# List matmuls ordered behind the dense products, the first listed unit one place later, and one modulation group moved from one block to the next

## The chip, the cores and the metric

The kernel runs on one core of one Trainium2 chip. The metric is the device time of one execution in microseconds; the profiled execution also gives a span, from the first to the last instruction of the trace.

## The reference, cut to what matters

Two layers on 256 positions of width 1024. Each layer is a mixer (layer 0 retention, layer 1 a spatial-gating unit) followed by a PEER expert retrieval over 128 x 128 experts. Every part has an adaptive modulation: six groups (shift, scale, gate, twice) that come from `c`.

```python
c_act = jax.nn.silu(c)
mod = c_act @ ada_w[layer] + ada_b[layer]
sh1, sc1, g1, sh2, sc2, g2 = jnp.split(mod, 6, axis=-1)   # groups 0 to 5
x = x + g1 * mixer(modulate(rmsnorm(x), sh1, sc1))
x = x + g2 * peer_ffn(modulate(rmsnorm(x), sh2, sc2), ...)
# peer_ffn: two top-16 lists per head give 16 experts of 16384 per head and token
a = gelu(einsum('tkd,td->tk', expert_u[idx], x)) * gate
return einsum('tk,tkd->td', a, expert_v[idx])
```

## The kernel before, in words

Float32 products are made of three matmuls each: an operand is split into `hi` (L162, ScalarE) and `lo = raw - hi` (L163, VectorE), and `hi*hi`, `hi*lo` and `lo*hi` are summed in PSUM. Weights come in tiles of 128 x 1024, loaded by SyncE's queue (L159) in a fixed order, `AHEAD = 2` tiles ahead of use, with three buffers for `raw`, `hi` and `lo`.

**PEER, up to the V products.** The 128 x 128 experts are held as 128 rows of 128. The activations of all experts are computed densely and multiplied by a dense table of gates. For the first `N0 = 72` rows the products go to a table in DRAM (`w_dram`, from tile `A`, in eight pieces); for the other 56 rows the activations go to `a_dram` and the gates stay in `G`.

**The V products.** They walk over 60 units (`peer_v_order`). 28 are natural: two whole expert rows, `at` reloaded from `a_dram` (L1051), multiplied by `G` (L1082), split into `wh` and `wl` (L1073, L1074), and 24 matmuls of 512 columns (L392). The other 32 are listed: expert cells that any token uses are packed into 64 columns; a unit of kind "b" (15) has 24 matmuls, of kind "x" (17) 12 (L1089). Each listed unit is fetched by four indirect DMAs from GpSimd (L168): two of `vraw` (weights) and two of `cell` (gated activations). They may run up to five units ahead (`DEEP + 1`). The first `FIRST = 16` units are natural, the remaining 12 are mixed among the listed ones, and one "b" comes last.

**The sorter.** Which cells are listed is worked out while the natural units run, by a generator `sort_rows`, of which each of the first `SORTED = 14` units advances one step: three steps of flags; masks, in a pool that takes the space of `A` and so waits until it was written out (`open_lists`, L915); `numbers`, with one matmul (L931) between VectorE operations; `lists`, with nine chunks of eight small matmuls (L984), each chunk needing `pm` and `eq` (L973, L977, VectorE), `cm` of its rows (L980, GpSimd) and of its columns (L982, ScalarE); then the indices `vi` and `agi` (L1018), which the gathers need; and a count (L1028, L1030) that SyncE and the other engines read for a branch (L1140). At unit 14 what is left of the sorter is emitted at once, and the gathers may begin.

**The modulation.** `ada(layer, ks)` is a generator that works out groups `ks`: for each group eight loads of 128 x 1024 (L287, SyncE's queue), eight VectorE operations (L289, L291), eight transposes on TensorE (L299) and two reductions (L300). It is advanced one step at a time between products. In layer 0's V products the groups (0,5), (1,1), (1,0) and (1,2) are made, in layer 1's group (1,5), and in layer 1's gating unit (1,4) and (1,3).

**The gating unit's output stage.** After the input projection (`z_group`) come `gate_rows(1, 2)`, which spreads group (1,2) over rows by eight VectorE operations `dg` (L375, two buffers) and eight transposes (L376), and then eight groups of spatial products (L207 to L209, `u` at L648), transposes (L658, `ph` and `pl` at L453, L454) and three output products each.

**Order.** The program's order is not the order on the engines: a scheduler simulates the program and places an instruction on its engine's queue when the simulation has it ready. `after_mark(inst, mark, ORDER)` keeps `inst` behind `mark` in that order, without a wait. `marks["pe"]` is the last product emitted so far. Engines then work through their queues in order.

Of the kernel before, what the change touches and what calls it, by code (L numbers as in the profile page):

```python
# [44 lines left out]
CAP = (17, 30, 17)  # L45
NC = sum(CAP)
BASE = (0, CAP[0], CAP[0] + CAP[1])
FIRST = 16
SORTED = 14
DEEP = 4  # L50


# [72 lines left out]
def trunk(ctx: ExitStack, tc: tile.TileContext, I, out):  # L125
# [449 lines left out]
    def sgu(xt, pool, update):  # L575
# [62 lines left out]
                nc.scalar.copy(vh[:, b, s], v)  # L638
                nc.vector.tensor_tensor(vl[:, b, s], v, f(vh[:, b, s]), op=ALU.subtract)
        accs = acc_tiles()  # L640
        filler = ada(1, (4, 3), hpool, "hl", "hh")

        def spatial(g):
            s = slice(g * GD, (g + 1) * GD)
# [16 lines left out]
                         ph[:, :, bs_], pl[:, :, bs_])  # L661
            return [(ph[:, e, :], pl[:, e, :]) for e in range(3)]

        grow = gate_rows(1, 2)
        spatial(0)
        spatial(1)
        nxt = turn(0)
        for g in range(GRP):
            if g + 2 < GRP:
                spatial(g + 2)  # L670
            cur, nxt = nxt, turn(g + 1) if g + 1 < GRP else None
            keys = [("sgu_out", g * 3 + e) for e in range(3)]
            if g == GRP - 1:
                drain(filler)
                out_group(accs, cur, keys)
            else:
                for e in range(3):
                    out_proj(accs, *cur[e], weight(*keys[e]), g == 0 and e == 0)
                    next(filler, None)
        return accs, grow  # L680

    def peer(layer, xt, hh, hl, xstack):
# [239 lines left out]
        def numbers(masks, caps, bases, pool, ps):  # L922

            n = len(caps)
            scan = pool.tile([P, n, n0], F32, tag="scan", name=nm("scan"))
            for c in range(n):
                nc.vector.tensor_tensor_scan(scan[:, c], ones[:, :n0], masks[:, c], 0.0,
                                             op0=ALU.mult, op1=ALU.add)
            sums = pool.tile([P, n], F16, tag="sums", name=nm("sums"))
            nc.vector.tensor_copy(sums, scan[:, :, n0 - 1])  # L930
            nc.tensor.matmul(ps[:, :n], listed["below"], sums, start=True, stop=True)  # L931
            off = pool.tile([P, n], F32, tag="off", name=nm("off"))
            nc.vector.tensor_copy(off, ps[:, :n])
            place = pool.tile([P, n0], F32, tag="place", name=nm("place"))
            left = pool.tile([P, n0], F32, tag="left", name=nm("left")) if n > 1 else None
            keep = pool.tile([P, n0], F32, tag="keep", name=nm("keep"))
            for c in range(n):
                pos = scan[:, c]
                nc.vector.tensor_scalar(pos, pos, off[:, c:c + 1], -1.0, op0=ALU.add, op1=ALU.add)
                nc.vector.scalar_tensor_tensor(keep, pos, float(caps[c] * P), masks[:, c],  # L940
                                               op0=ALU.is_lt, op1=ALU.mult)
                dst = place if c == 0 else pos
                nc.vector.scalar_tensor_tensor(dst, pos, float((bases[c] + 1) * P), keep,
                                               op0=ALU.add, op1=ALU.mult)
                if c:
                    nc.vector.tensor_tensor(place, place, pos, op=ALU.add)
                if n == 1:
                    continue
                d2 = left if c == 0 else keep
                nc.vector.tensor_tensor(d2, masks[:, c], keep, op=ALU.subtract)  # L950
                if c:
                    nc.vector.tensor_tensor(left, left, keep, op=ALU.add)
            return place, left

        def lists(place, ncol, pool, ps):

            ip = pool.tile([P, n0], U32, tag="ip", name=nm("ip"))
            iq = pool.tile([P, 2, n0], U32, tag="iq", name=nm("iq"))
            ih = pool.tile([P, 2, n0], F16, tag="ih", name=nm("ih"))
            nc.vector.tensor_copy(ip, place)  # L960
            nc.vector.tensor_scalar(iq[:, 0], ip, 127, None, op0=ALU.bitwise_and)
            nc.vector.tensor_scalar(iq[:, 1], ip, 7, None, op0=ALU.logical_shift_right)
            nc.vector.tensor_copy(ih, iq)
            yield
            ps = ps[:, :2 * ncol].rearrange("p (v c) -> p v c", v=2)

            def pairs(row, width):
                return row.rearrange("p (q e) -> p q e", e=2).unsqueeze(2) \
                    .to_broadcast([P, 4, width, 2])

            for i in range(0, n0, 8):
                pm = pool.tile([P, 4, P, 2], F16, tag="pm", bufs=2, name=nm("pm"))
                nc.vector.tensor_tensor(pm, iota_h.unsqueeze(1).to_broadcast([P, 4, P, 2]),  # L973
                                        pairs(ih[:, 0, i:i + 8], P), op=ALU.is_equal)
                cm = pool.tile([P, 4, 2, ncol, 2], F16, tag="cm", bufs=2, name=nm("cm"))
                eq = pool.tile([P, 4, ncol, 2], F16, tag="eq", bufs=1, name=nm("eq"))
                nc.vector.tensor_tensor(  # L977
                    eq, listed["cols"][:, :ncol].unsqueeze(1).to_broadcast([P, 4, ncol, 2]),
                    pairs(ih[:, 1, i:i + 8], ncol), op=ALU.is_equal)
                nc.gpsimd.tensor_tensor(cm[:, :, 0], eq, pairs(listed["rows"][:, i:i + 8], ncol),  # L980
                                        op=ALU.mult)
                nc.scalar.mul(cm[:, :, 1], eq, pidx)  # L982
                for k in range(8):
                    nc.tensor.matmul(ps, pm[:, k // 2, :, k % 2], cm[:, k // 2, :, :, k % 2],  # L984
                                     start=i + k == 0, stop=i + k == n0 - 1)
                yield
            row = pool.tile([P, ncol], F32, tag="row", name=nm("row"))
            nc.vector.tensor_copy(row, ps[:, 1])
            nc.vector.scalar_tensor_tensor(row, ps[:, 0], float(P), row, op0=ALU.mult, op1=ALU.add)
            v = pool.tile([P, ncol], I32, tag="vi", name=nm("vi"))  # L990
            nc.vector.tensor_scalar(v, row, float((layer * P - 1) * P), 0.0,
                                    op0=ALU.add, op1=ALU.max)
            yield row, v

        def sort_rows():
            for i in range(0, n0, 24):
                flag(1, i, 15, nc.vector)
                flag(1, i + 15, 9, nc.scalar)
                yield
            code, second = flags  # L1000
            nc.vector.tensor_scalar(second, second, 0.0, 2.0, op0=ALU.is_gt, op1=ALU.mult)
            nc.vector.scalar_tensor_tensor(code, code, 0.0, second, op0=ALU.is_gt, op1=ALU.add)
            open_lists()
            lp = listed["pool"]
            masks = lp.tile([P, 3, n0], F32, name=nm("masks"))
            for k, value in enumerate((1.0, 3.0, 2.0)):
                nc.vector.tensor_scalar(masks[:, k], code, value, None, op0=ALU.is_equal)
            yield
            place, left = numbers(masks, CAP, BASE, lp, ps_tile())
            yield  # L1010
            for got in lists(place, NC, lp, ps_tile()):
                yield
            row, listed["v"] = got
            agi = lp.tile([P, NC], I32, name=nm("agi"))
            one, two, three = (slice(BASE[c], BASE[c] + CAP[c]) for c in range(3))
            nc.vector.tensor_scalar(agi[:, one], row[:, one], 2.0, None, op0=ALU.mult)
            nc.vector.tensor_copy(agi[:, two], row[:, two])
            nc.vector.tensor_scalar(agi[:, three], row[:, three], 2.0, 1.0,  # L1018
                                    op0=ALU.mult, op1=ALU.add)
            listed["w"] = agi  # L1020
            yield
            listed["left"] = left
            count = lp.tile([P, 1], F32, name=nm("count"))
            nc.vector.tensor_reduce(count, left, axis=AX.X, op=ALU.add)
            ch = lp.tile([P, 1], F16, name=nm("ch"))
            nc.vector.tensor_copy(ch, count)
            ps = ps_tile()
            nc.tensor.matmul(ps[:1, :2], ch, ones_h, start=True, stop=True)  # L1028
            ci = lp.tile([1, 2], I32, name=nm("ci"))
            nc.vector.tensor_copy(ci, ps[:1, :2])  # L1030
            listed["count"] = ci
            yield

        accs = acc_tiles()
        if layer == 0:
            adag = chain(ada(0, (5,), hpool, "hl", "hh"), ada(1, (1, 0, 2), hpool, "hl", "hh"))
        else:
            adag = ada(1, (5,), hpool, "hl", "hh")
        order = peer_v_order()
# [83 lines left out]
        for pos, unit in enumerate(order):  # L1123
            wh, wl = nxt
            kind, c = unit
            if pos < SORTED:
                next(sorter, None)
            elif pos == SORTED:
                drain(sorter)
                listed["rows_pool"] = vstack.enter_context(  # L1130
# [148 lines left out]
```

## Time and profile before

| | |
|---|---|
| time, median of 3 runs | 2169.87 us (2166.07 to 2176.35) |
| time of the profiled execution | 2171.77 us |
| its span | 2170.0 us |
| TensorE matmul busy | 1993.5 us (92%) |
| VectorE busy | 1685.8 us (78%) |
| ScalarE, GpSimd busy | 1121.7 us (52%), 571.1 us (26%) |
| mean granted TensorE clock | 0.964 of full |

The page gives busy time per engine as a share of the span. "PE" is TensorE's matmuls, "PEld" its weight loads, "DVE" VectorE, "ACT" ScalarE, "POOL" GpSimd, "SP" SyncE; a "q" behind an engine is its sequencer or DMA queue. A wait is idle time of an engine, put down to what ended it. Line numbers are those of the kernel before.

### The profile page before, as it was taken

To read this page: it belongs to the slowest core of one execution; us is meant where nothing else is said; L and a number is where in the kernel's file an instruction comes from. 1 tells how busy PE (TensorE), PEld (TensorE's weight loads), DVE (VectorE), ACT (ScalarE), POOL (GpSimd) and SP (SyncE) were. 2 spreads that over 40 slices of the span, in tenths; PEclk is the share of its full clock that TensorE was granted. 3 is DMA by queue.
4 is the path that set the end of the run, shared out by engine and by line. 5 is a ranking of instruction groups with operands and counts; after the bars stand their busy time and mean duration, and the time that the engine had idled before them with its cause. 6 is when DMAs were issued, how large, how long until landed. Compare 5 with 4: busy or idle time off the path is not lost. (4 is left out here: it accounts for less than half of the span.)

```text
span 2170.0 us, 35151 instructions
## 1 busy us (share of the span) xinstructions
PE 1993.5 (92%) x12988; PEld 1777.3 (82%) x12988; DVE 1685.8 (78%) x3064; ACT 1121.7 (52%) x1894; POOL 571.1 (26%) x523
## 2 busy tenths in 40 slices
PE   4999899999999598899889899999999995988997
PEld 4988799999989476677677787999999894766785
DVE  7877678988988676678678777789989886666675
ACT  3444444446887444445454434444467874444553
POOL 1000001101010435877001700011010104448770
PEclk8999999999999799999999999999999997999999
DMA  7677456665575677899646865566555756777893
GB/s 267 213 256 263 162 177 185 183 183 183 181 248 190 228 233 256 277 335 357 214 154 214 256 230 189 176 182 183 184 181 189 247 189 230 233 246 241 299 299 111
DMA packets 137019, 478.72 MB, mean 221 GB/s; under 512 B 17408, under 2 KB 19472, under 8 KB 136320
## 3 DMA queue, kind: packets, MB, share of 16 engines
q1 hardware_dynamic: 94320, 335.85, 48.0%
q0 software_dynamic: 38192, 131.04, 18.2%
q10 hardware_dynamic: 4320, 9.44, 1.2%
q8 instruction: 105, 1.72, 0.3%
q14 instruction: 82, 0.67, 0.1%
HBM read 439.30 MB, written 36.96 MB: 219 GB/s over the span
## 5 line engine op out<-in xcount | busy, mean ns | idle before, releaser
L162 ACT CAST hi<-raw 128x1024 fp32r<-128x1024 f32 x536 | 561.5, 1049 | 643.4 <-PE ps L208 337.4
L163 DVE TENSOR_TENSOR lo<-raw,hi 128x1024 fp32r<-128x1024 f32 x536 | 683.1, 1277 | 123.8 <-ACT hi L162 121.0
L207 PE MATMUL ps<-hh,hi 128*128 128x256 f32 x2432 | 699.3, 288 | 11.6 <-ACT hi L162 7.8
L208 PE MATMUL ps<-hl,hi 128*128 128x256 f32 x2432 | 691.7, 285 | 1.6 <-DVE hl L358 1.4
L209 PE MATMUL ps<-hh,lo 128*128 128x256 f32 x2432 | 691.1, 285 | 1.7 <-DVE lo L163 1.5
L207 PEld LDWEIGHTS ps<-hh,hi 128*128 128x128 f32 x2432 | 468.7, 193 | 13.5 <-ACT hi L162 8.5
L208 PEld LDWEIGHTS ps<-hl,hi 128*128 128x128 f32 x2432 | 468.9, 193 | 2.4 <-DVE hl L358 2.4
L209 PEld LDWEIGHTS ps<-hh,lo 128*128 128x128 f32 x2432 | 468.3, 193 | 2.6 <-DVE lo L163 2.6
L163 DVE TENSOR_TENSOR lo<-vraw,hi 128x1024 fp32r<-128x1024 f32 x128 | 156.1, 1225 | 98.2 <-ACT hi L162 97.8
L392 PE MATMUL acc<-lo,wh 128*128 128x512 f32 x672 | 217.1, 404 | 4.8 <-DVE lo L163 4.7
L162 ACT CAST hi<-vraw 128x1024 fp32r<-128x1024 f32 x128 | 134.1, 1050 | 152.5 <-DMA vraw<-in_peer_v,vi 78.7
L392 PE MATMUL acc<-hi,wl 128*128 128x512 f32 x672 | 210.8, 395 | 0.0
L392 PE MATMUL acc<-hi,wh 128*128 128x512 f32 x672 | 193.5, 402 | 4.9 <-ACT wh L1073 3.3
L168 POOL DMA_INDIRECT cell<-w_dram,agi x128 | 167.3, 1307 | 39.0 <-issue 33.5
L759 POOL TENSOR_TENSOR eq<-eq,tif 128x512 f32<-128x512 f32 x32 | 56.7, 1786 | 449.8 <-DVE eq L754 403.8
L168 POOL DMA_INDIRECT vraw<-in_peer_v,vi x128 | 145.9, 1140 | 73.2 <-DVE agi L1018 33.6
L392 PEld LDWEIGHTS acc<-hi,wh 128*128 128x128 f32 x672 | 126.6, 190 | 35.7 <-ACT wh L1073 3.5
L392 PEld LDWEIGHTS acc<-lo,wh 128*128 128x128 f32 x672 | 124.1, 190 | 36.9 <-DVE lo L163 10.3
L392 PEld LDWEIGHTS acc<-hi,wl 128*128 128x128 f32 x672 | 126.1, 188 | 30.2
L907 POOL DMA_DIRECT2D a_dram<-at x56 | 30.6, 546 | 374.6 <-ACT at L802 228.8
L208 PE MATMUL ps<-lo,hh 128*128 128x512 f32 x320 | 125.8, 393 | 3.4 <-DVE lo L163 3.4
L209 PE MATMUL ps<-hi,hl 128*128 128x512 f32 x320 | 125.6, 392 | 0.0
(275 smaller groups left out, 2844.5 us busy)
## 6 DMA issues: line engine op xcount, KB each, us to landing
raw<-in_peer_u SPq DMA_DIRECT2D x256, 512.0 KB, 3.7
raw<-in_peer_v SPq DMA_DIRECT2D x112, 512.0 KB, 4.9
adaw<-in_ada_w SPq DMA_DIRECT2D x96, 512.0 KB, 5.3
raw<-in_sgu_in SPq DMA_DIRECT2D x48, 512.0 KB, 4.6
w_dram<-A POOLq DMA_DIRECT2D x16, 1152.0 KB, 14.4
raw<-in_ret_vg SPq DMA_DIRECT2D x32, 512.0 KB, 4.4
raw<-in_peer_q SPq DMA_DIRECT2D x32, 512.0 KB, 3.7
a_dram<-at POOLq DMA_DIRECT2D x56, 256.0 KB, 3.4
```

The source lines that it names most:

```text
L162: after_mark(nc.scalar.copy(hi, raw), after[0], ORDER)
L163: after_mark(nc.vector.tensor_tensor(lo, raw, f(hi), op=ALU.subtract), after[1], ORDER)
L168: nc.gpsimd.indirect_dma_start(out=dst, out_offset=None, in_=table, in_offset=bass.IndirectOffsetOnAxis(ap=index, axis=0))
L207: first = nc.tensor.matmul(ps, ah, bh, start=start, stop=False)
L208: nc.tensor.matmul(ps, ah, bl, start=False, stop=False)
L209: marks["pe"] = nc.tensor.matmul(ps, al, bh, start=False, stop=stop)
L392: marks["pe"] = nc.tensor.matmul(accs[b][n], a[:, tb], bb[:, n * 512:(n + 1) * 512], start=first and a is lh and bb is wh, stop=False)
L759: nc.gpsimd.tensor_tensor(eq, eq, tif[:, :, a, :].unsqueeze(2).to_broadcast([P, NTB, TOPK, TOPK]), op=ALU.mult)
L907: nc.gpsimd.dma_start(a_dram[:, sp * 2:sp * 2 + 2, :], tmp)
```

## The change

`FIRST` becomes 17 and `SORTED` 13: 17 natural units stand ahead of the first listed one, eleven are mixed among them, and the gathers are emitted from unit 13 on. The sorter takes two steps instead of one at units 5, 7, 9 and 11. The matmul of `numbers`, that of the count and the first of each chunk of the lists are kept behind the last dense product emitted before them; a chunk's matmuls are emitted in the step after the one that prepares its operands. `cm` of the rows moves from GpSimd to VectorE, and `eq` gets a second buffer. Group (1,2) leaves layer 0's V products and becomes the first of three groups in layer 1's output stage, with one more step behind most groups, and `gate_rows(1, 2)` moves from ahead of the spatial products to the end of output group 2.

```diff
-FIRST = 16
-SORTED = 14
+FIRST = 17
+SORTED = 13
...
-        filler = ada(1, (4, 3), hpool, "hl", "hh")
+        filler = ada(1, (2, 4, 3), hpool, "hl", "hh")
...
-        grow = gate_rows(1, 2)
         spatial(0)
         spatial(1)
...
                     out_proj(accs, *cur[e], weight(*keys[e]), g == 0 and e == 0)
                     next(filler, None)
+                    if e == 2 and g == 2:
+                        grow = gate_rows(1, 2)
+                    elif e == 2 and g:
+                        next(filler, None)
...
-            nc.tensor.matmul(ps[:, :n], listed["below"], sums, start=True, stop=True)
+            after_mark(nc.tensor.matmul(ps[:, :n], listed["below"], sums, start=True, stop=True),
+                       marks["pe"], ORDER)
...
-                eq = pool.tile([P, 4, ncol, 2], F16, tag="eq", bufs=1, name=nm("eq"))
+                eq = pool.tile([P, 4, ncol, 2], F16, tag="eq", bufs=2, name=nm("eq"))
...
-                nc.gpsimd.tensor_tensor(cm[:, :, 0], eq, pairs(listed["rows"][:, i:i + 8], ncol),
+                nc.vector.tensor_tensor(cm[:, :, 0], eq, pairs(listed["rows"][:, i:i + 8], ncol),
                                         op=ALU.mult)
                 nc.scalar.mul(cm[:, :, 1], eq, pidx)
+                yield
                 for k in range(8):
-                    nc.tensor.matmul(ps, pm[:, k // 2, :, k % 2], cm[:, k // 2, :, :, k % 2],
-                                     start=i + k == 0, stop=i + k == n0 - 1)
-                yield
+                    after_mark(nc.tensor.matmul(
+                        ps, pm[:, k // 2, :, k % 2], cm[:, k // 2, :, :, k % 2],
+                        start=i + k == 0, stop=i + k == n0 - 1),
+                        marks["pe"] if k == 0 else None, ORDER)
...
-            nc.tensor.matmul(ps[:1, :2], ch, ones_h, start=True, stop=True)
+            after_mark(nc.tensor.matmul(ps[:1, :2], ch, ones_h, start=True, stop=True),
+                       marks["pe"], ORDER)
...
-            adag = chain(ada(0, (5,), hpool, "hl", "hh"), ada(1, (1, 0, 2), hpool, "hl", "hh"))
+            adag = chain(ada(0, (5,), hpool, "hl", "hh"), ada(1, (1, 0), hpool, "hl", "hh"))
...
             if pos < SORTED:
-                next(sorter, None)
+                for _ in range(1 + (pos > 3 and pos % 2)):
+                    next(sorter, None)
```

## Rows read from the trace of the kernel before

**Rows 1.** Waits of PE over the whole span, longest in total: us, times, longest.
```profile
PE ps L931 <- DVE sums L930: 25.8, 2, 12.9
PE ps L984 <- POOL cm L980: 17.9, 2, 8.9
PE acc L1089 <- ACT wh L1073: 15.1, 2, 7.7
```

**Rows 2.** Stages: busy us (x instructions) of each engine, PE clock, DMA share, GB/s.
```profile
722.00:746.00 24.00, 1.27 (x10) 1.03 (x10) 11.47 (x41) 3.98 (x6) 5.92 (x7) 0.59 0.77 282
746.00:842.00 96.00, 95.87 (x445) 74.33 (x446) 67.30 (x70) 42.95 (x52) 38.10 (x36) 0.98 0.65 205
842.00:1072.00 230.00, 208.69 (x868) 161.39 (x867) 174.10 (x190) 112.51 (x134) 153.56 (x127) 0.96 0.89 310
980.00:1040.00 60.00, 59.40 (x259) 47.66 (x259) 50.41 (x55) 34.10 (x40) 41.26 (x37) 1.00 1.00 368
1928.00:2140.00 212.00, 193.72 (x808) 152.03 (x808) 138.54 (x153) 107.11 (x128) 153.81 (x127) 0.96 0.80 271
1250.00:1328.00 78.00, 76.86 (x365) 63.32 (x365) 61.08 (x74) 29.96 (x40) 0.00 (x0) 0.99 0.69 230
```

**Rows 3.** Timeline of all engines at the start of layer 0's V products.
```profile
732.49 0.29 DVE L915 TENSOR_SCALAR below<-iota_f,pidx 128x128 f16<-128x128 f32 x1 [11.17 <-DMA w_dram<-A]
733.91 0.55 POOL L1051 DMA_DIRECT2D at<-a_dram  x1 [11.06 <-DMA a_dram<-at]
...
741.89 1.42 POOL L980 TENSOR_TENSOR cm<-eq,rows_h 128x512 f16<-128x512 f16 x1 [5.40 <-DVE eq L977]
...
743.27 1.26 POOL L1082 TENSOR_TENSOR at<-at,G 128x512 f32<-128x512 f32 x1
...
745.48 0.60 ACT L1073 CAST wh<-at 128x512 fp32r<-128x512 f32 x1
...
746.13 1.22 PE L392 MATMUL acc<-hi,wh 128*128 128x512 f32 x2 [1.67 <-ACT wh L1073]
```

**Rows 4.** Tile `at`, 730 to 775 us: issue to landing of its loads.
```profile
DMA to landing us min/median/max: 2.9/3.0/4.1
```

**Rows 5.** Timeline of PE, 829 to 862 us: a list chunk, the gathers' wait.
```profile
831.05 0.63 PE L984 MATMUL ps<-cm,pm 128*128 128x128 f16 x8
831.49 0.71 PE L392 MATMUL acc<-hi,wh 128*128 128x512 f32 x2
832.04 0.63 PE L392 MATMUL acc<-lo,wh 128*128 128x512 f32 x2
832.50 0.62 PE L392 MATMUL acc<-hi,wl 128*128 128x512 f32 x2
...
850.36 1.22 PE L1089 MATMUL acc<-hi,wh 128*128 128x512 f32 x2 [7.43 <-ACT wh L1073]
...
861.46 0.63 PE L1089 MATMUL acc<-hi,wh 128*128 128x512 f32 x2
```

**Rows 6.** Timeline of POOL: first and last of layer 0's 128 gathers.
```profile
836.87 1.04 POOL L168 DMA_INDIRECT vraw<-in_peer_v,vi  x1 [16.30 <-DVE agi L1018]
...
1032.47 0.94 POOL L168 DMA_INDIRECT vraw<-in_peer_v,vi  x1 [0.30 <-issue]
```

**Rows 7.** Tile `eq`: VectorE's operation on it, ns min/median/max.
```profile
L977 DVE TENSOR_TENSOR eq<-cols_h,ih x18: 410/425/1518, 741.4 to 1903.1; 128x512 f16<-128x512 f16 x18
```

**Rows 8.** Waits of PE, 840 to 1070 us: us in total, times, longest.
```profile
PE acc L1089 <- ACT hi L162: 4.7, 2, 4.2
```

**Rows 9.** Waits of SP's queue, 700 to 760 us.
```profile
SPq L1140 <- DVE ci L1030: 6.3, 1, 6.3
```

**Rows 10.** Timeline, 1236 to 1262 us: PE at the gating unit's output stage.
```profile
1242.35 0.48 PE L376 MATMUL ps<-ident,dg 128*128 128x128 f32 x1 [5.11 <-DVE dg L375]
...
1250.13 1.22 PE L392 MATMUL acc<-hi,ph 128*128 128x512 f32 x2
```

**Rows 11.** VectorE's groups, shapes apart, 1237 to 1328 us: busy us, mean ns.
```profile
L291 DVE SCALAR_TENSOR_TENSOR ada<-adaw,c_act,ada 128x1024 f32<-128x1024 f32 x14 | 17.9, 1281 | 2.9 <-DMA adaw<-in_ada_w 1.8 <-PE ps L209 1.0
```

## The prediction, as it was put on record

> **What bounds the kernel now.** I read the page first: TensorE is busy for 92% of the span, so only stretches in which it stands still, and changes of its clock, can pay. The list of TensorE's waits comes next [rows 1]: three of its longest belong to the lines of this change, each twice, once a layer, and nearly alike in both layers (half of each total is about its longest). So I work out layer 0 and carry it to layer 1. The stage windows then say which parts of the V products have slack. Between the last u product and the first dense product TensorE is busy for 1.3 of 24 us; while the natural units run it is full (95.9 of 96 us); in the part with listed units it idles 21.3 of 230 us in layer 0 and 18.3 of 212 us in layer 1 [rows 2]. What the lists cost inside the full part therefore matters, and what hides beside it doesn't.
>
> The timeline of the start shows why TensorE waits. VectorE is held until 732.5 us by the write of `A`, and the reload of the first natural unit is issued at 733.9. It takes 3.0 us to land [rows 4], so its data are there at 736.9. But GpSimd does the first list chunk's `cm` at 741.9 before it multiplies the reload by `G` at 743.3, and TensorE has the matmul of `numbers` and the first eight list matmuls in its queue ahead of the products; the first product starts at 746.1 [rows 3]. At the other end, the gathers begin at 836.9 us, when `agi` is ready, and the first gathered product starts at 850.4, 13.5 us later, after a wait of 7.4 us and at half rate (1.22 us for two matmuls, where two later take 0.63: TensorE's lower clock level, 1.2 GHz, instead of 2.4; the granted clock averages 0.59 over the idle start) [rows 2, 5, 6].
>
> **The start of the V products.** Afterwards TensorE's queue holds the products of four units ahead of `numbers`, and GpSimd has no `cm`. The chain of the first product is then the load (736.9), the multiplication by `G` (1.26, to 738.2) and the cast `wh` (0.60, to 738.8): start at 738.9, 7.2 us earlier [rows 3, 4]. VectorE is free from 732.5, more than four microseconds before the reload lands, for the masks and the `lo` of the first rows; I take that as no bound. The eight list matmuls that ran in the idle time now stand among the products, where a chunk takes 0.44 us (831.05 to 831.49) [rows 5]. Gain 6.8 us a layer, 13.5 in all; nothing at the lower end, if the order on VectorE or GpSimd keeps list work ahead.
>
> **The first gathers.** A unit of 24 products takes 5.6 us (two per 0.46 to 0.47 us [rows 5]). Seventeen units, 72 list matmuls (9 x 0.44 = 4.0) and a half-rate start that costs 3.7 (before, 16 units and eight chunks make 93.1 us and took 96.8, from 746.1 to the 842.9 that lies 7.4 ahead of 850.4 [rows 3, 5]) end at 738.9 + 95.2 + 4.0 + 3.7 = 841.8. The ninth list chunk is emitted in unit 11's steps, behind the products of 11 units: its own matmuls and the eight before it included, 738.9 + 61.6 + 3.7 + 4.0 = 808.2. Before, 5.4 us lay between the end of the last chunk and the first gather (831.5 to 836.9); so gathers start at about 813.6, 28 us ahead of use instead of 6. They need 13.5, so the wait goes, and with it the half rate behind it: 850.36 to 861.46 holds one "x" and one "b", 36 products, 8.4 us at full rate, so 2.7 are lost [rows 5]. Gain 7.4 + 2.7 in layer 0 and 7.7 + 2.7 in layer 1 [rows 1]: 20.5.
>
> **The rest of the listed part.** In layer 0, 21.3 - 7.4 = 13.9 us of idle time are left, in layer 1 18.3 - 7.7 = 10.6 [rows 1, 2]; the largest is a wait for a gathered row's `hi` (4.7 us in two waits) [rows 8]. GpSimd issues 128 gathers from 836.9 to 1033.4 without a pause: 1.53 us each, 6.1 us a listed unit [rows 6]. TensorE needs 5.6 us for a "b" and 2.8 for an "x", and only the 12 natural units between them give GpSimd time: 15 x 5.6 + 17 x 2.8 + 12 x 5.6 = 199 us against 196. The two are even, so GpSimd can't make up a late start, and 15 us more of lead (28 less 13.5) cover as much of the lateness. Half-rate stretches behind the longest waits add some 2.5 us a layer, by the one above. I take 60% of 16.4 in layer 0, where the DMA share is 0.89, and 75% of 13.1 in layer 1, where it is 0.80 [rows 2]: 9.8 + 9.8 = 19.6. The bounds are nothing and 29.5.
>
> **What a list chunk costs now.** On VectorE `cm` is an operation of the size of `eq`, 0.42 us alone and up to 1.52 beside GpSimd's work [rows 7]: 9 x 0.42 = 3.8 us a layer, or 13.7. VectorE is busy for 67 of 96 us there [rows 2], so both fit. I take the lower, since GpSimd loses the work that it would collide with. The Trainium skill ("GPSIMD Engine Reference", section "8. Key points") says that GpSimd shares its memory interfaces with VectorE when VectorE has two inputs in SBUF, which speaks against a move to an engine with no interface of its own; the trace bears it out in the 1518 ns beside the 410 [rows 7]. By that rule alone the sum would hold 13.7 us a layer of VectorE time, still hidden.
>
> Where a unit takes two steps, a chunk's matmuls are held only behind the products that held the chunk before it, and TensorE may reach them before `cm` is there: three chunks a layer, at most about 4.4 us each, nothing at best. (The 4.4 are an estimate: two operations of 1.5 [rows 7], and 0.7 each for `pm`, twice as wide as `eq`, and for ScalarE's part.) Natural products queue behind it. In the full part before, eight chunks cost no wait [rows 2], so I take 0.5 each, 3 us. The count now becomes ready 13 units later, and SyncE's read of it (6.3 us before, in the idle start [rows 9]) holds the row loads behind it. Rows are loaded about three ahead, so I take 0.5 a layer, 1 us; 6.3 at the worst. One natural unit more is reloaded through ScalarE's queue and multiplied on VectorE: hidden. New waits: 4 us.
>
> **The moved group.** Eight loads of 512 KB, eight VectorE operations, eight transposes and two reductions leave layer 0's listed part and enter layer 1's output stage; TensorE's share is equal on both sides. In layer 0 it is 4.2 MB less, which is why I go to 60% above. In the output stage the first product runs at 1250.1, behind a wait of 5.1 us for a `dg` that sits in VectorE's queue behind the last weights, and at half rate [rows 10]. Without `gate_rows` there it can start some 5.5 us earlier. But VectorE is busy for 61 of the 78 us that follow [rows 2], and gets eight operations of 1.28 [rows 11], two reductions and the eight `dg`: 10 us and, as an estimate from these operations' smaller sizes, 4 more, so 75 of about 73 to 78. It becomes as long as TensorE's own work, and its waits give back the gain. I take nothing, with 6 us either way.
>
> **Sum.** 13.5 + 20.5 + 19.6 - 4 + 0 = 49.6 us. From the profiled execution's 2171.8 that is 2122; it lies 1.9 above the median of the runs, so the forecast is 2121.
>
> **Rivals.** *The transfers bind the listed part.* With TensorE at full rate (980 to 1040 us) the DMA engines are busy all the time, at 368 GB/s [rows 2]. Then an earlier start only makes the same bytes wait elsewhere, and the 19.6 are lost: 2121 + 20 = 2141. For it speaks that share; against it, that layer 0 loses 4.2 MB and layer 1 ran at 271 GB/s with almost as much idle time. The Trainium skill ("DMA: Bandwidth & Descriptors", section "Issuing engines are not separate DMA queues") has this rule: transfers of all queues run on the same 16 engines and interleave. The trace agrees, with a share of 1.00.
>
> *The output stage becomes VectorE's.* If its bursts can't be hidden, TensorE waits for most of the added 14 us, less the 5.5: about 9 us worse, 2130. A gap of 1.6 us stands there even now (78 - 76.9 [rows 2]).
>
> *The list matmuls hold the products* (the other side). TensorE works in order; if the scheduler places each chunk where its `cm` is only being prepared, all 18 wait. At 4.4 us each that is 79 us, less the 53.6 gained: 2170 + 25 = 2195. From 3 us each it is slower than before. Against it: none did so in the full part before.
>
> *It doesn't do what it says.* The order binds only TensorE's queue; VectorE's and GpSimd's may still put list work ahead, and the start stays, while the fetches go no further ahead than before: 2160 to 2172.
>
> **Chances and range.** The forecast 0.56, the transfers 0.17, the output stage 0.13, no effect 0.07, the list matmuls 0.07. The forecast's own range is 2101 (all of the 29.5, no new wait, 6 us in the output stage) to 2130; the range takes in the first two rivals to 2149, with a few us of new waits on top. Less than 0.5%, some 11 us, can't be told from no change here. Faster by more: 0.86; within: 0.08; slower: 0.06.
>
> **What would show it.** In the profile after: the first dense product about 5 us behind the reload's issue instead of 12; the first list matmul behind four units; no wait of L1089 for `wh`; `agi` some 28 us ahead of the first gathered product; GpSimd waiting for buffers between gathers, a sign that it leads. Against it: waits of TensorE for `cm` in the full part; the same idle time behind the first gathered unit at a DMA share near 1; VectorE above 95% in the output stage with TensorE waiting for `u`, `pl` or `lo`.

## The result, and the profile after

The changed kernel takes 2108.8 us (median of 4 runs, 2107.36 to 2110.9) against 2170.79 us for the kernel before on the same chip (4 runs, 2166.07 to 2176.35): ratio 0.9714, 95% interval 0.9689 to 0.974. It is 62 us faster; 49.6 were forecast. Two runs, one of e11 below (2146.47 us) and one of the kernel before on the same chip (2204.12 us), lay over 1.5% above the fastest run of their kernel and are left out.

I cut both traces at four landmarks, so that each stretch holds one idea of the change: the first dense V product of either layer, the first matmul of the norm (L337) that follows layer 0, and the same for the norm between the gating unit and the second PEER part.

| stretch, us | before | after | gain |
|---|---|---|---|
| start to first V product, layer 0 | 746.1 | 737.6 | 8.5 |
| V products, layer 0, to the next norm | 349.0 | 315.8 | 33.2 |
| gating unit, norm to norm | 241.4 | 251.3 | -9.9 |
| PEER of layer 1 up to its first V product | 495.1 | 487.5 | 7.6 |
| V products, layer 1, to the end | 338.4 | 315.5 | 22.9 |
| span | 2170.0 | 2107.7 | 62.3 |

TensorE's longest wait of the changed kernel over the whole span, in us, times, longest, answers to [rows 1]:

```profile
PE acc L392 <- ACT wh L1080: 34.8, 2, 17.4
```

The three waits have become one, for the first `wh` of each layer. No wait for `numbers` or for `cm` is left, and for gathered weights only 1.0 us in two waits, for their `lo`. The timeline of the start, which answers to [rows 3], shows the new chain:

```profile
731.30 0.29 DVE L918 TENSOR_SCALAR below<-iota_f,pidx 128x128 f16<-128x128 f32 x1 [11.18 <-DMA w_dram<-A]
...
732.71 0.55 POOL L1058 DMA_DIRECT2D at<-a_dram  x1 [11.07 <-DMA a_dram<-at]
...
735.63 1.26 POOL L1089 TENSOR_TENSOR at<-at,G 128x512 f32<-128x512 f32 x1 [0.34 <-DMA at<-a_dram]
736.92 0.62 ACT L1080 CAST wh<-at 128x512 fp32r<-128x512 f32 x1 [9.49 <-POOL at L1089]
...
737.59 1.22 PE L392 MATMUL acc<-hi,wh 128*128 128x512 f32 x2 [17.41 <-ACT wh L1080]
```

The first product follows 4.9 us behind the reload's issue, where it took 12.2. GpSimd multiplies the reload as soon as it lands.

The next view is the V products by stage, layer 0 in three windows and layer 1 in three; it answers to [rows 2] and has its columns (us, busy us of PE, PEld, DVE, ACT and POOL, then the clock, the DMA share and GB/s).

```profile
737.60:841.00 103.40, 100.90 (x474) 79.78 (x474) 80.17 (x115) 48.68 (x59) 51.59 (x43) 0.98 0.76 256
841.00:1020.00 179.00, 177.03 (x764) 141.74 (x764) 147.96 (x164) 98.82 (x118) 138.33 (x110) 0.99 0.92 333
1020.00:1053.40 33.40, 24.54 (x108) 19.20 (x106) 20.49 (x34) 15.06 (x23) 1.14 (x2) 0.94 0.31 97
...
1792.20:1890.00 97.80, 97.75 (x463) 78.15 (x464) 75.82 (x113) 46.59 (x56) 56.62 (x40) 0.98 0.75 253
1890.00:2080.00 190.00, 187.80 (x808) 149.32 (x807) 137.12 (x151) 106.08 (x127) 135.28 (x113) 1.00 0.82 280
2080.00:2107.70 27.70, 13.70 (x58) 10.45 (x56) 14.89 (x30) 6.91 (x13) 1.68 (x3) 0.81 0.16 59
```

The part with listed units is full now: TensorE stands still for 2.0 of 179 us in layer 0 and 2.2 of 190 in layer 1, at a clock of 0.99 and 1.00. The transfers are no bound there: their share is 0.92 beside a TensorE that is busy for 177.03 of 179 us.

GpSimd's first and last gather of layer 0 [rows 6], then TensorE where the listed units begin [rows 5]:

```profile
810.47 1.04 POOL L168 DMA_INDIRECT vraw<-in_peer_v,vi  x1 [13.04 <-DVE agi L1024]
...
1009.38 1.97 POOL L168 DMA_INDIRECT vraw<-in_peer_v,vi  x1 [0.30 <-DMA vraw<-in_peer_v,vi]
```

```profile
839.99 1.19 PE L392 MATMUL acc<-hi,wh 128*128 128x512 f32 x4 [2.45 <-ACT hi L162]
841.25 1.22 PE L392 MATMUL acc<-lo,wh 128*128 128x512 f32 x2
...
844.71 1.08 PE L1096 MATMUL acc<-hi,wh 128*128 128x512 f32 x4
845.63 0.63 PE L1096 MATMUL acc<-lo,wh 128*128 128x512 f32 x2
```

From the start of the first to the start of the last the 128 gathers take 198.9 us, nearly the pace of before (195.6 us). They only start 26 us earlier, 34 us ahead of the first gathered product. A wait of 2.45 us for a row's `hi` is new, just ahead of the listed units.

The gating unit's output stage [rows 10] is the one part that lost:

```profile
1247.45 0.66 PE L376 MATMUL ps<-ident,dg 128*128 128x128 f32 x2 [3.74 <-DVE dg L375]
...
1289.76 0.49 PE L208 MATMUL acc<-lo,ph 128*128 128x512 f32 x1 [1.80 <-DVE lo L163]
...
1297.50 1.06 PE L299 MATMUL ps<-ident,ada 128*128 128x128 f32 x8
1304.71 5.75 PE L337 MATMUL ps<-diag,x 128*128 128x128 f32 x32 [6.14 <-DVE diag L326]
```

### The profile page after: what moved, and what is told of

Read it like the earlier page. It is cut to its first block, busy times and chain, and to the rows that moved or that the text cites. A ratio compares the mean times of both kernels' runs of the same rounds, so it can differ in the third digit from the quotient of the medians.

```text
span 2107.7 us, 35151 instructions
## 1 busy us (share of the span) xinstructions
PE 1972.6 (94%) x12988; PEld 1769.4 (84%) x12988; DVE 1682.0 (80%) x3084; ACT 1122.2 (53%) x1894; POOL 564.6 (27%) x501
## 5 line engine op out<-in xcount | busy, mean ns | idle before, releaser
L168 POOL DMA_INDIRECT vraw<-in_peer_v,vi x128 | 157.9, 1234 | 57.2 <-issue 26.5
L168 POOL DMA_INDIRECT cell<-w_dram,agi x128 | 158.9, 1241 | 39.0 <-issue 35.0
## 6 DMA issues: line engine op xcount, KB each, us to landing
w_dram<-A POOLq DMA_DIRECT2D x16, 1152.0 KB, 14.4
```

What stands on the lines that cost most here:

```text
L168: nc.gpsimd.indirect_dma_start(out=dst, out_offset=None, in_=table, in_offset=bass.IndirectOffsetOnAxis(ap=index, axis=0))
```

## The experiments

My theory after reading this trace: the V products' gain is real and has three parts (the start, the gathers' lead, the idle time and half-rate stretches between listed units), and the moved group nets nothing, because what layer 0 gains the output stage loses. The rivals were that the moved group frees the transfers and so carries part of the gain, and that one of order, early lists or `cm`'s engine does all of it. Each run has one trace, so equal code tells what a stretch of a trace scatters by: the gating unit with `gate_rows` ahead and two groups takes 241.4 to 244.8 us in six traces (before, e1, e3, e4, e7, e8), and layer 0's V products 323.5 and 327.9 us in e1 and e5.

**The changed kernel without the moved group** (`e1_v_only`):

```diff
-        filler = ada(1, (2, 4, 3), hpool, "hl", "hh")
+        filler = ada(1, (4, 3), hpool, "hl", "hh")
+        grow = gate_rows(1, 2)
         spatial(0)
...
-                    if e == 2 and g == 2:
-                        grow = gate_rows(1, 2)
-                    elif e == 2 and g:
-                        next(filler, None)
...
-ada(1, (1, 0), hpool, "hl", "hh"))
+ada(1, (1, 0, 2), hpool, "hl", "hh"))
```

> The changed kernel with the moved group put back: group (1,2) is made in layer 0's V products again, and its gate rows stand ahead of the spatial products. Theory: the parts that touch the V products give some 50 of the 62 us by themselves, the move gives about 9 to 13 us at the end of layer 0's V products and costs about 10 in layer 1's output stage, so this kernel is near the changed one, 2107 to 2115 us, with the output stage (first output product to the next norm's first matmul) back at about 86 us instead of 101 and waits at the branch that ends layer 0's V products back. Rival: the listed part of layer 0 was held by its transfers, and only the 4.2 MB less freed it: then the idle time behind the first gathered unit comes back in layer 0, 2122 to 2130 us.

Measured: 2113.02 us, ratio 0.9734 (0.9707 to 0.976); that overlaps the changed kernel's interval. Its listed part in layer 0, in the columns of the stage windows:

```profile
835.00:1030.00 195.00, 192.18 (x828) 152.41 (x827) 162.82 (x175) 107.55 (x128) 134.74 (x111) 1.00 0.92 330
```

With the group's 4.2 MB still there, TensorE is as full as in the changed kernel (190.53 of the same 195 us, at a share of 0.89). So the transfers do not bind this part. The gating unit takes 241.4 us as before. But layer 0's V products take 323.5 us instead of 315.8, and TensorE's timeline shows where, at the end of the layer:

```profile
1036.74 1.06 PE L299 MATMUL ps<-ident,ada 128*128 128x128 f32 x8 [1.82 <-DVE ada L291]
...
1039.18 0.69 PE L376 MATMUL ps<-ident,dg 128*128 128x128 f32 x2 [1.15 <-DVE dg L375]
...
1045.09 0.77 PE L207 MATMUL acc<-hi,wh 128*128 128x512 f32 x1 [4.58 <-PEq L1145]
```

The fourth group is still unfinished when the products end, `gate_rows` follows it, and the branch on the count (L1145 here) then holds TensorE for 4.6 us.

**The moved group alone** (`e2_move_only`): the kernel before with the same lines changed the other way.

> The kernel before with nothing but the moved group and gate rows. Theory: about 9 to 13 us gained at the end of layer 0's V products, about 10 lost in the output stage: 2162 to 2174 us, no change that can be told. Rival (transfers): the listed part of layer 0 loses its waits behind the first gathered unit, 2150 to 2158 us.

Measured: 2172.28 us, ratio 1.0002 (0.9988 to 1.0017). No change, made of two halves: layer 0's V products gain 14.4 us (349.0 to 334.6), the gating unit loses 9.8 (241.4 to 251.2); the rest is scatter of the stretches between.

**The order alone** (`e3_order_only`): the kernel before with `after_mark` at the three matmuls and the `yield` ahead of a chunk's matmuls.

> The kernel before with nothing but the order edges and the later emission of a chunk's matmuls; one step a unit, 16 natural units first, cm on GpSimd. Theory: the first dense product starts about 7 us earlier in both layers and nothing else moves, since agi is still ready only at the end of the natural units: 2154 to 2160 us, the wait ahead of the first gathered product still there. Rival (list matmuls hold the products): TensorE waits for cm in the full part, 2165 us or more.

Measured: 2159.69 us, ratio 0.9955 (0.9927 to 0.9984). The first V product comes at 737.71 us as in the changed kernel, so the start needs the order and nothing else. The wait for the first gathers is still there, in TensorE's waits over the span (L1093 is the listed product):

```profile
PE acc L1093 <- ACT wh L1077: 14.3, 3, 7.3
```

**Everything of the V part but the order** (`e4_early_only`): the kernel before with

```diff
-FIRST = 16
-SORTED = 14
+FIRST = 17
+SORTED = 13
...
-tag="eq", bufs=1
+tag="eq", bufs=2
...
-nc.gpsimd.tensor_tensor(cm[:, :, 0]
+nc.vector.tensor_tensor(cm[:, :, 0]
...
-                next(sorter, None)
+                for _ in range(1 + (pos > 3 and pos % 2)):
+                    next(sorter, None)
```

> The kernel before with everything that makes the gathers early (17 natural units first, fetches from unit 13, double steps, cm on VectorE with two eq buffers) and no order edge. Theory: the start of the V products stays as it was (the matmul of numbers and the first list chunk ahead of the products), and the waits ahead of and behind the first gathered unit mostly go: 20 us and 15 to 25 us, 2125 to 2136 us. Rival: without the order the scheduler pulls more list chunks ahead of the products, and the start gets later by what the gathers gain: 2145 us or more.

Measured: 2129.35 us, ratio 0.9808 (0.978 to 0.9836). The gathers' wait is gone; the start stays, as TensorE's waits show:

```profile
PE ps L931 <- DVE sums L930: 25.8, 2, 12.9
PE ps L984 <- DVE cm L980: 21.5, 2, 10.8
```

`cm` comes from VectorE here, and TensorE waits as long: at the start it was never GpSimd's speed, but that list work stood ahead of the products. Order and early lists give 0.45% and 1.92% alone and 2.66% together (e1), so they add up, within their intervals.

**The order with the old constants** (`e8_late`): `e1_v_only` with `FIRST = 16`, `SORTED = 14` and one step of the sorter for each unit.

> The kernel with the V parts, but FIRST 16, SORTED 14 and one step a unit again: order edges, cm on VectorE and two eq buffers alone. Theory: the earlier steps and the 17th unit are what gives the gathers their lead, so the wait ahead of the first gathered product comes back, and most of what lay behind it: like the kernel with order alone, 2150 to 2160 us. Rival: cm on VectorE by itself gets agi ready earlier: 2125 to 2140 us.

Measured: 2150.46 us, ratio 0.9906 (0.9879 to 0.9933), and the wait for gathered weights is back in TensorE's waits:

```profile
PE acc L1093 <- ACT wh L1077: 9.3, 2, 5.0
```

So the extra natural unit, the gathers from unit 13 on and the double steps are worth 37 us (2150.46 less 2113.02) once the lists are ordered behind the products; they are the larger half of the change.

**`cm` back on GpSimd** (`e7_cm_pool`): `e1_v_only` with

```diff
-tag="eq", bufs=2
+tag="eq", bufs=1
...
-nc.vector.tensor_tensor(cm[:, :, 0]
+nc.gpsimd.tensor_tensor(cm[:, :, 0]
```

> The kernel with the V parts alone, but cm of the rows on GpSimd again and one buffer of eq. Theory: with the order edges the chunks come late enough that GpSimd has done the first units' products, so cm's engine hardly matters: the same start of the products, agi a few us later, within 5 us of 2113: 2110 to 2118 us. Rival: cm on GpSimd comes late behind the reloads (GpSimd works in order and waits for each reload), TensorE waits for it in the full part: 2122 us or more.

Measured: 2130.74 us, ratio 0.9819 (0.9783 to 0.9854): 18 us, more than the 5 that I had allowed, and in the rival's range. GpSimd's first gathers start at, in layer 0 and layer 1,

```profile
815.34 1.04 POOL L168 DMA_INDIRECT vraw<-in_peer_v,vi  x1 [7.03 <-DVE agi L1021]
...
1878.91 1.04 POOL L168 DMA_INDIRECT vraw<-in_peer_v,vi  x1 [8.95 <-DVE agi L1021]
```

Counted from each layer's first product, they start 5.4 and 6.8 us later than in e1 (808.01 and 1863.13). But that is not what costs the time: the first gathered product comes later too, so the lead stays at 34.0 and 32.2 us (32.3 and 31.4 in e1), and TensorE waits for no gathered `wh`. The time goes ahead of it, among the natural units. Layer 1 from its first product to the first gathered one, in e1 and then in e7, and a wait of e7's TensorE in the same part of layer 0:

```profile
1791.70:1894.50 102.80, 102.74 (x482) 81.69 (x483) 82.23 (x117) 49.86 (x60) 58.50 (x43) 0.98 0.79 265
```

```profile
1800.70:1911.10 110.40, 104.52 (x482) 81.01 (x483) 84.76 (x108) 49.30 (x60) 62.78 (x52) 0.98 0.74 247
```

```profile
796.97 0.63 PE L986 MATMUL ps<-cm,pm 128*128 128x128 f16 x8 [1.57 <-DVE pm L974]
```

TensorE idles there for 5.9 us instead of 0.1, and in layer 0 for 4.8 instead of 0.5 (110.4 us long, against 103.4). It waits for the `pm` of a list chunk (1.6 and 1.4 us), for `cm` (0.4) and for the `hi` and `lo` of rows. `eq`, with one buffer again, waits on VectorE for GpSimd's `cm` (0.9 and 1.9 us), and what stands behind it in VectorE's queue comes later. How much is the engine and how much the missing buffer was not separated, and some of it can be scatter: e5, with the same V parts as e1, takes 103.9 and 107.6 us there. Up to the next norm layer 0 takes 3.5 us more than in e1, which shows nothing, since e5 takes 4.4 more; layer 1 takes 8.2 more up to the branch behind its last product. Another 5.4 fall behind that branch, in an idle time of 2.7 us that nothing in the trace ends and half-rate products after it; what it is stays open, and so do the few us elsewhere.

**Two groups, but `gate_rows` at output group 2** (`e5_gate_g2`): `e1_v_only` with

```diff
-        grow = gate_rows(1, 2)
         spatial(0)
...
                     next(filler, None)
+                    if e == 2 and g == 2:
+                        grow = gate_rows(1, 2)
```

> The kernel with the V parts alone (group (1,2) still made in layer 0), but with its gate rows at the end of output group 2. It tells the place of the gate rows from the third modulation group in the output stage. Theory: the place by itself gains the 4 to 5 us of the wait for dg at the head of the stage, and what cost 10 us was the third group's loads and VectorE operations: norm to norm 236 to 239 us (241.4 with the V parts alone, 251.3 with the whole change), time 2106 to 2111 us. Rival: the gate rows in the middle of the stage are what stalls (TensorE waits there for dg): 245 to 249 us, 2116 to 2121 us.

Measured: 2106.72 us, ratio 0.9706 (0.9679 to 0.9732); the gating unit takes 237.7 us, against 241.4 with `gate_rows` ahead and 251.3 with the third group as well. So the third group costs 13.6 us, and the later gate rows gain 3.7, little more than the stretch scatters by.

**What in the third group costs it.** In `e9_no_vec` seven of its eight VectorE operations are left out, in `e10_no_load` seven of its eight loads, each from the changed kernel:

```diff
+                elif (layer, k) == (1, 2):
+                    yield
+                    continue
                 else:
                     op = nc.vector.scalar_tensor_tensor(
```

```diff
-                w = pool.tile([P, 1024], F32, tag=wtag, bufs=bufs, name=nm("adaw"))
-                loads.append(nc.sync.dma_start(w, I["ada_w"][layer, k, dc]))
+                if (layer, k) != (1, 2) or dc == 0:
+                    w = pool.tile([P, 1024], F32, tag=wtag, bufs=bufs, name=nm("adaw"))
+                    loads.append(nc.sync.dma_start(w, I["ada_w"][layer, k, dc]))
```

> The changed kernel with seven of the eight VectorE operations of the moved group (1,2) left out; its eight loads, eight transposes and two reductions stay, so the gate rows of the spatial unit's mixer hold wrong numbers. The stretch from the first norm matmul behind layer 0 to the norm-2 matmul of layer 1 took 251.3 us with the group and 241.4 without. Theory (VectorE's operations are what the third group costs): 7 x 1.28 = 9 us less for VectorE, the stretch falls to 240 to 245, time some 2100 us. Rival (its 4.2 MB of loads cost it, beside the weights of the output projection): the stretch stays at 249 to 252, time within 3 us of the changed kernel's 2109.

> The changed kernel with seven of the eight loads of group (1,2) left out: its VectorE operations stay and all read the first tile, so the numbers of the group are wrong. Theory (VectorE): the stretch between the two norms stays at 248 to 252 us, time 2106 to 2110. Rival (the loads): it falls to 240 to 245, time some 2100.

In `e11_spread` group 0 advances the modulation at every product twice (`elif e == 2 or g == 0:` for `elif e == 2 and g:`), so that it ends before the last output group.

> The changed kernel with three more steps of the modulation in output group 0, so that the third group is done before the last output group instead of behind its last product (1296.1 to 1298.6 us, and a wait of 6.1 us for the norm's diag instead of 3.7). Theory (that tail is a part of the 10 us that the third group costs): the stretch between the norms falls from 251.3 to 247 to 249.5, time some 2106. Rival (VectorE is late in the whole stage, and an earlier burst only moves the waits): it stays at 250.5 to 255, time 2108 to 2113.

Measured: 2123.51, 2137.05 and 2116.15 us; the kernel before scattered from 2166.15 to 2195.35 us on the chip of these three, so I read the stretch between the norms and not the times. (Layer 0's V products, the same code in all three, take 329.4, 327.5 and 314.9 us, and in e9 hold an idle time of 7.2 us that nothing in the trace ends.) The stretch is 245.2 us without the VectorE operations (1066.45 to 1311.68), 253.3 without the loads (1065.70 to 1319.04), and 248.1 with the steps spread (1053.61 to 1301.72). So the loads are not the cost. The VectorE operations account for some 6 of the third group's 13.6 us, and the group's late end for some 3.5: from the start of the last product to the norm TensorE takes 7.6 us in the changed kernel (1297.09 to 1304.71) and 4.1 in e11 and e5. In e9 the late end is still there, with a wait of 6.14 us for the norm's `diag`, as in the changed kernel, so these are two separate costs. In e11 the wait is 3.7 us, as with two groups (TensorE's timeline of e11). Some 4 us of the 13.6 stay open.

```profile
1301.72 3.81 PE L337 MATMUL ps<-diag,x 128*128 128x128 f32 x32 [3.73 <-DVE v L279]
```

Whether e11 beats the changed kernel in time is not settled (ratio 0.9695, 0.9584 to 0.9806).

**A group moved elsewhere** (`e6_ret_gz`): `e1_v_only` with group (0,5) in retention's filler, one step more for each head, and `gate_rows(1, 2)` in the gating unit's input projection.

```diff
-ada(0, (2, 4, 3), pool, "ada", "adaw", 2)
+ada(0, (2, 4, 3, 5), pool, "ada", "adaw", 2)
...
-            fill(2)
+            fill(3)
...
             if n == 8:
                 spatial_weights()
+            if n == 9:
+                grow = gate_rows(1, 2, g=pool.tile([P, D], F32, tag="grow"))
```

> A version meant to beat both: the V parts, with group (0,5) made in layer 0's retention (three filler steps instead of two in each of eight places) so that layer 0's V products still have three groups, not four, as in the changed kernel, two groups in layer 1's output stage, and the gate rows of (1,2) made during the input projection, in a tile of their own. Theory: the 7.7 us at the end of layer 0's V products are kept, the 10 us in the output stage are not paid and its head gains 4 to 5: 2092 to 2101 us, if the retention hides nine more steps. Rival: retention becomes VectorE's (it is 80% busy there): up to 10 us lost, 2102 to 2110 us.

Measured: 2119.09 us, ratio 0.9762 (0.9735 to 0.9789): not faster than e1, whose interval it overlaps, and above both ranges that I had given. The gating unit takes 239.7 us, less by no more than its scatter. The V products of layer 0 take 315.7 us, as the moved group makes them, but the first one comes at 759.0 us instead of 737.0: retention was full (50.00 of 50 us in the changed kernel), and isn't any more:

```profile
110.00:160.00 50.00, 44.81 (x202) 36.54 (x201) 37.28 (x64) 21.47 (x33) 2.18 (x4) 0.97 0.71 226
160.00:200.00 40.00, 37.68 (x171) 30.69 (x170) 29.14 (x44) 15.67 (x23) 2.03 (x2) 0.96 0.81 272
```

## Why the prediction was right, and where its sum was off

The 49.6 us of the sum against the traces, term by term:

| | forecast | measured |
|---|---|---|
| start of the V products, both layers | 13.5 | 14.7 |
| layer 0: first gathers, rest, new waits | 10.1 + 9.8 - 2 | 33.2 |
| layer 1: first gathers, rest, new waits | 10.4 + 9.8 - 2 | 22.9 |
| output stage | 0 | -9.9 |
| other | 0 | 1.4 |
| sum | 49.6 | 62.3 |

**The start** was right in mechanism and size. From the last u product to the first V product it took 25.0 us, and now 17.7, in both layers. e3 shows that the order alone does it.

**The first gathers** were right. Their waits of 7.4 and 7.7 us are gone, and the lead came out at 34 us where I had worked out 28. e8 brings the waits back with nothing but the old constants and steps. The sign that I had named, GpSimd waiting for buffers between gathers, did not show: no gap between two gathers is longer than 0.31 us, and of the 34 us of lead 30 are left at the last gather (1009.38, for the last unit's products from 1039.71). In the kernel before the lead grew, from 13.5 to 46 us (1032.47 to 1078.60), because TensorE stood waiting.

**The rest of the listed part** was mis-sized. I took 19.6 us, with 29.5 at most. Beyond the first waits, idle time fell by 10.8 us in layer 0 (from 20.2 to 2.0 us in the window up to 1060 and 1020 us, less 7.4) and by 8.4 in layer 1 (from 18.3 to 2.2, less 7.7): some four fifths of what was left (12.8 and 10.6 us) in both layers, not 60 and 75%. The half rate was sized further off, in layer 0 above all. From a layer's first V product to its end TensorE's busy time fell by 11.4 us in layer 0 (313.89 to 302.47, some 1 us of it the moved transposes) and by 6.3 in layer 1 (305.56 to 299.24), where I had counted 2.7 and 2.5 us a layer at most; the clock of the listed windows rose from 0.96 to 0.99 and 1.00. The 60% rested on the share of the transfers, and that step failed: e1, with all the bytes still in layer 0, is as full. The Trainium skill ("DMA: Bandwidth & Descriptors", section "Issuing engines are not separate DMA queues") says that transfers of all queues interleave on the same 16 engines. No run here tells the queues apart on an engine; what e1 shows is a share of 0.92 beside a TensorE that is busy for 192.18 of 195 us. A high share alone did not make a bound.

**Layer 0's end** is what I missed. The kernel before, TensorE's timeline, and behind it the same place of the changed kernel:

```profile
1073.30 0.33 PE L376 MATMUL ps<-ident,dg 128*128 128x128 f32 x1 [1.49 <-DVE dg L375]
...
1078.60 0.77 PE L207 MATMUL acc<-hi,wh 128*128 128x512 f32 x1 [4.97 <-PEq L1140]
```

```profile
1039.71 0.47 PE L207 MATMUL acc<-hi,wh 128*128 128x512 f32 x1 [1.03 <-PEq L1148]
```

Between the last listed units and the next norm, TensorE idled for 14.9 us in before (1060 to 1095.1, 20.19 busy) and for 8.9 after (1020 to 1053.4, 24.54 busy), and ran at a clock of 0.80 against 0.94. I had read the windows up to 1072 us and the waits up to 1070, and so cut off this wait. It hangs on the fourth group: 4.6 to 5.1 us in all seven kernels that make four groups there (before, e1, e3, e4, e5, e7, e8), 1.0 to 1.2 in the six that make three. Why the sequencer needs longer there stays open.

**New waits**, 4 us, came out at 3.4 us, but not as the waits that I had named. In TensorE's waits of the changed kernel they are, at 839.99 and 1892.85 us, ahead of the listed units:

```profile
PE acc L392 <- ACT hi L162: 3.4, 2, 2.4
```

No wait for `cm` came, and none of SyncE for the count at the start; later it waited 1.3 us for `ci` in layer 0, and whether a row came late for that is not shown. `cm` on VectorE takes 414 ns at the median and 1546 at most, as bounded by [rows 7], and VectorE hides it. What the sum has nowhere is what `cm` would have cost on GpSimd (1359 ns at the median) with one buffer of `eq`: 18 us in e7, where TensorE waits for chunks and rows among the natural units.

**The output stage** failed: I took nothing, and the rival "the output stage becomes VectorE's" had its size (9 us worse forecast, 9.9 measured). The gain at its head was there: counted from the previous V part's end, the first output product came 4.4 us earlier. But 14 us were lost behind it, 13.6 by the third group (e5): some 6 by its VectorE operations (e9) and some 3.5 by its end behind the last product (e11). So the rival's mechanism is right in part only: VectorE was busy for 80.73 of 100 us there, not above 95%; it was late at single places, not full. My test by VectorE's sum could not have told it.

The two misses hide each other: the moved group gains 8 to 14 us in layer 0 and costs 10 in the gating unit, and alone it is worth nothing (e2). That the sum came within 13 us is luck to that extent: both layers' V products gave 20 us more than forecast, and the output stage 10 less. What remains of the measured time is the V part's. Added one after another, the order gives 0.45% (e3), `cm` on VectorE with the second `eq` 0.5% more (e8, whose interval meets that of e3), and the lead of the lists another 1.7% (e1).

## What to carry to other kernels

Work that prepares a later stage belongs behind the products that can already run, and its result early enough that the later stage's slowest feeder starts with a lead: a feeder as fast as its consumer makes up a late start only by the consumer's waits, but keeps most of a lead that it is given. When filler work is moved out of a full stage, look at the end of the old stage (what is still unfinished behind the last product) and at the end of the new one: the price lies there and in single late operations, and the busy sum of the helping engine does not show it. Read waits up to the next landmark, not to a round number.

## What the runs showed of the hardware that was not expected

The branch on a loaded count behind layer 0's V products cost TensorE 4.6 to 5.1 us in seven kernels, where matmuls that waited for VectorE stood just before it, and 1.0 to 1.2 us in six, where products did; that the waits are the cause is not shown. An operation on 128 x 512 float16 took 1359 ns on GpSimd (e7) and 414 ns on VectorE (the changed kernel), both at the median, in the same stage. And GpSimd issued its 128 gathers at 1.53 to 1.57 us each, from start to start, in both layers of both kernels, whether TensorE waited for them or not.
